# Three of seven pairs of up blocks with both blocks by seven block products

## The chip, the cores and the metric

The kernel runs on one core of one Trainium2 chip. The metric is the device time of the whole program in microseconds (us); the median over several executions is compared. Engines are named as in the profile: PE (TensorE matmul), PEld (its weight load), DVE (VectorE), ACT (ScalarE), POOL (GpSimd), SP (SyncE, which only issues transfers here).

## The reference

One decoder layer on x of 512 tokens by 1024 features: a mixer (four mLSTM heads and a group of convolutions with a common output projection), then a gated feed-forward part, each between norms that are modulated from the vector c (the "ada" weights). The change lies in the feed-forward part:

```python
u = rms_norm(x, ffn_pre_g[l]) * (1.0 + sc2) + sh2
up = causal_dwconv(u @ ffn_up[l], ffn_conv_w[l], ffn_conv_b[l])      # D_FF = 2816, conv width 3
a, gt = jnp.split(up, 2, axis=-1)
f = (jax.nn.silu(gt) * a) @ ffn_down[l]
x = x + g2 * rms_norm(f, ffn_post_g[l])
```

All of it is float32.

## The kernel before, in words

A float32 product is made of three fast ones: each operand is split into a rounded part (hi) and the rest (lo), and PE runs hi x hi, hi x lo and lo x hi into the same sum. So one 128 x 128 tile of weights against 512 tokens costs three matmuls.

**Up blocks.** The 2816 features of each half of up make 22 blocks of 128. Up block n computes value block n and gate block n for all 512 tokens. A plain block takes 2 halves x 8 tiles x 3 = 48 matmuls of 512 columns (plain_half, lines 188 to 190). Blocks 0 to 7 are plain. Blocks 8 to 21 run in seven pairs, m = 4 to 10, with i = 2m and j = 2m + 1. Of each pair the even block i is computed by a scheme with seven products in place of eight: its weights form a 2 x 2 arrangement (value and gate against the two halves of the 1024 features), its tokens two halves, and seven products p1 to p7 of 12 matmuls of 256 columns each (form_product, L1095) are made of sums of weight quarters and sums of token parts. first_products makes four: p1 in the left and p5 in the right half of a bank X, p7 in Z, p6 in W. between(i) then combines them: two ACT copies (L1111 of X, L1112 of W) and four DVE additions in PSUM (L1113 to L1116). last_products_up adds p2 and p3 to X and p4 to Z. The odd block j is plain: its value half runs between the first four and the last three products of i, its gate half behind them.

**Weights.** up_load fetches the quarters of a block (256 KB each) through SP's queue into one of two raw buffers, wups0 for even and wups1 for odd blocks. A form of a weight is split in one of two ways. w_split: ACT copies the rounded part (L170), POOL subtracts it from the source (L171). added_split: ACT writes the rounded part and its negative (L1086, L1087), and a transfer that POOL issues adds the source to the latter in memory (L1088). The forms of the even block are made in place in the raw quarters by DVE subtractions and additions (before: L1316 for p3, L1349 for p7, L1350 for p5, L1365 for p6), so each of them must wait until the form that was there is split. All splits take tiles of one pool, w, of 20.

**After the products.** conv3 convolves a half over tokens (L997 on ACT, L999 on DVE), unit_out makes F = value x silu(gate) (L1141 ACT, L1142 DVE), form_sums (L1024 to L1027), form_highs (L1032) and form_lows (L1038) prepare F of the pair before for the down products. ada_fetch and ada_add (L1146, L1151) put four blocks of the last modulation into pairs 5 to 8; four more (L153, L155) run ahead of the up blocks. After pair 8 ada_done (L160) and gain (L667) finish that modulation.

**Order.** In the pairs nothing is reordered: the code is under in_order(), so that DVE, ACT and POOL each run their instructions in the order in which the loop issues them, and PE and SP always do. An engine that waits at one instruction holds up all behind it. PE's banks: four for X and Z or plain blocks ("mm"), two for W ("at"), two for plain halves of j ("cv").

**Down products** follow with the same scheme; at the end last_products(2) and (3) make the last p4 of blocks m = 8, 9, 10 for the two token halves q (prod2, L1465), whose weight forms t_8, t_9, t_10 are split just ahead (L1015, L1016).

## Time and profile before

| | us |
|---|---|
| three executions | 768.56, 769.04, 771.67 (median 769.04) |
| the profiled execution | 769.46 |
| its span, first to last instruction | 767.7 |
| PE busy in the span | 753.0 |
| first matmul of pair 8/9 to that of pair 10/11 (528.76 to 549.76) | 21.00 |

The rows of the profile come from one execution: start and duration in us, engine, line, operation, tile names, and in brackets the idle time ahead with what ended it. The groups and the page give totals. The first matmul of a pair is told by the tile upx. Mean granted clock of PE is 0.997.

### The profile page before, as it was taken

The numbers are of one execution on the slowest core, as the hardware profiler recorded it, in microseconds if no ns is written. First come the engines' busy times: TensorE is split into PE (matmuls) and PEld (weight loads), VectorE is DVE, ScalarE is ACT, GpSimd is POOL, SyncE is SP. The second block draws the span as 40 slices with busy tenths as digits, with TensorE's granted clock in tenths as the row PEclk, the third lists the DMA queues.
The fourth block names the chain that finished last, engine by engine and source line by source line (L and its number), as shares of the span: only waits on it lengthen the run. The fifth ranks groups of instructions, "written<-read, shape, count | busy, mean of one in ns | idle before, by whom it ended". The sixth has DMA issues, their size and how long they took to land.

```text
span 767.7 us, 11547 instructions
## 1 busy us (share of the span) xinstructions
PE 753.0 (98%) x3961; PEld 644.1 (84%) x3961; DVE 640.2 (83%) x1034; ACT 449.9 (59%) x860; POOL 367.2 (48%) x320
## 2 busy tenths in 40 slices
PE   7999999999999999999999999999999999999996
PEld 5778898778888888988888998889998988888884
DVE  6997999999999966765768789877787878999986
ACT  5448257676766547582244566677676667546653
POOL 2029578696798735433661435455565554100001
PEclk9999999999999999999999999999999999999998
DMA  8983214203123453334953679899788879899692
GB/s 322 370 309 122 102 55 165 82 29 127 61 86 112 138 183 118 139 117 155 382 180 129 241 186 237 204 251 231 207 202 194 214 204 225 258 356 373 225 335 109
DMA packets 55999, 148.47 MB, mean 193 GB/s; under 512 B 6370, under 2 KB 7810, under 8 KB 51844
## 3 DMA queue, kind: packets, MB, share of 16 engines
q1 hardware_dynamic: 33588, 100.37, 37.9%
q10 hardware_dynamic: 14288, 32.68, 12.3%
q0 software_dynamic: 8064, 14.68, 11.1%
q8 instruction: 31, 0.51, 0.3%
q14 instruction: 28, 0.23, 0.1%
HBM read 117.42 MB, written 15.61 MB: 173 GB/s over the span
## 4 chain that ended last, share of the span: by engine, by line
PE 67%; DVE 22%; DMA 6%; ACT 2%; issue 2%; POOL 1%; ACTq 0%; DVEq 0%; POOLq 0%; SPq 0%
DVE cv L731 10%; PE up L190 7%; PE up L189 7%; PE up L188 7%; PE upx L1095 4%; PE glu L189 3%; PE glu L190 3%; PE glu L188 3%; PE p L1465 3%; PE p L189 3%; PE p L188 3%; PE p L190 3%; PE upz L1095 2%; PE mixa L188 2%; PE mixa L190 2%
## 5 line engine op out<-in xcount | busy, mean ns | idle before, releaser
L731 DVE SCALAR_TENSOR_TENSOR cv<-gt,cvw,cv 128x505 f32<-128x505 f32 (+24 forms) x200 | 137.3, 729 | 2.3 <-ACT cv L719 1.1
L727 POOL TENSOR_TENSOR cs<-cs,cs 128x510 f32<-128x510 f32 (+3 forms) x32 | 41.8, 1306 | 0.3
L685 POOL TENSOR_TENSOR ro2r<-ro2t,mhalf 128x1 f32<-128x1 f32 x1 | 0.6, 562 | 82.7 <-DVE ro2t L683 82.7
L725 ACT ACTIVATE cs<-gt,cvw 128x511 f32<-128x511 f32 (+4 forms) x40 | 27.5, 720 | 5.9 <-POOL cs L727 2.7
L155 DVE SCALAR_TENSOR_TENSOR junk<-ada,cb 128x1024 bf16<-128x1024 f32 x16 | 24.9, 1559 | 7.2 <-DMA ada<-in_adaT 7.0
L189 PE MATMUL up<-u2l,wup_0h 128*128 128x512 f32 (+1 forms) x72 | 25.7, 356 | 0.2 <-DVE u2l L910 0.2
L188 PE MATMUL up<-u2h,wup_0h 128*128 128x512 f32 (+1 forms) x72 | 25.6, 356 | 0.0
L190 PE MATMUL up<-u2h,wup_0l 128*128 128x512 f32 (+1 forms) x72 | 25.4, 353 | 0.0
L171 POOL TENSOR_TENSOR wglu_0l<-wglu,wglu_0h 128x512 fp32r<-128x512 f32 x4 | 5.5, 1382 | 41.3 <-PE glu L190 41.3
L171 POOL TENSOR_TENSOR wqko_1024l<-wqko,wqko_1024h 128x512 fp32r<-128x512 f32 x12 | 15.6, 1296 | 18.3 <-ACT wqko_1024h L170 12.9
L155 DVE SCALAR_TENSOR_TENSOR junk<-spare,cb 128x1024 bf16<-128x1024 f32 x12 | 18.6, 1548 | 4.1 <-DMA spare<-in_adaT 3.9
L188 PE MATMUL qko<-uh,wqko_1024h 128*128 128x512 f32 x48 | 20.6, 430 | 0.0
L188 PE MATMUL qko<-uh,wqko_0h 128*128 128x512 f32 x48 | 20.2, 420 | 0.0
L276 DVE SCALAR_TENSOR_TENSOR junk<-ada,cb 128x1024 bf16<-128x1024 f32 x16 | 19.5, 1220 | 0.1
L171 POOL TENSOR_TENSOR wo_512l<-wo,wo_512h 128x512 fp32r<-128x512 f32 x8 | 12.9, 1614 | 13.7 <-PE mixa L189 11.5
L171 POOL TENSOR_TENSOR wqko_0l<-wqko,wqko_0h 128x512 fp32r<-128x512 f32 x12 | 16.6, 1384 | 4.9 <-ACT wqko_0h L170 4.9
L190 PE MATMUL qko<-uh,wqko_1024l 128*128 128x512 f32 x48 | 18.8, 392 | 0.0
L171 POOL TENSOR_TENSOR wqko_512l<-wqko,wqko_512h 128x512 fp32r<-128x512 f32 x12 | 17.0, 1419 | 3.7 <-ACT wqko_512h L170 3.7
L190 PE MATMUL qko<-uh,wqko_0l 128*128 128x512 f32 x48 | 18.8, 391 | 0.0
L171 POOL TENSOR_TENSOR wo_1024l<-wo,wo_1024h 128x512 fp32r<-128x512 f32 x8 | 11.7, 1456 | 14.9 <-ACT wo_1024h L170 14.9
L189 PE MATMUL qko<-ul,wqko_1024h 128*128 128x512 f32 x48 | 18.7, 390 | 0.0
L189 PE MATMUL qko<-ul,wqko_0h 128*128 128x512 f32 x48 | 18.7, 390 | 0.0
(1239 smaller groups left out, 3118.5 us busy)
## 6 DMA issues: line engine op xcount, KB each, us to landing
wups<-in_w_up SPq DMA_DIRECT2D x56, 256.0 KB, 4.8
wqko<-in_w_qko SPq DMA_DIRECT2D x12, 1024.0 KB, 4.7
ada<-in_adaT ACTq DMA_DIRECT2D x20, 512.0 KB, 4.4
ada<-in_adaT SPq DMA_DIRECT2D x16, 512.0 KB, 6.8
wo<-in_w_out SPq DMA_DIRECT2D x8, 1024.0 KB, 4.8
wup<-in_w_up SPq DMA_DIRECT2D x8, 1024.0 KB, 6.9
spare<-in_adaT ACTq DMA_DIRECT2D x12, 512.0 KB, 7.6
wd<-in_w_down SPq DMA_DIRECT2D x20, 256.0 KB, 5.7
```

The costliest lines, as they stand in the source:

```text
L155: t = V.scalar_tensor_tensor(out=junk, in0=r, scalar=1.0, in1=cb, op0=ALU.mult, op1=ALU.mult, accum_out=mod[:, i : i + 1])
L171: (eng or G).tensor_tensor(out=lo[:, :n], in0=src, in1=hi[:, :n].bitcast(F32), op=ALU.subtract)
L188: PE.matmul(ps, a[0], b[0], start=start, stop=False)
L189: PE.matmul(ps, a[0], b[1], start=False, stop=False)
L190: PE.matmul(ps, a[1], b[0], start=False, stop=stop)
L276: V.scalar_tensor_tensor(out=junk, in0=first[k][:, i * D : (i + 1) * D], scalar=1.0, in1=cb, op0=ALU.mult, op1=ALU.mult, accum_out=part[k] ...
L685: G.tensor_tensor(out=r, in0=t, in1=mhalf[:, :1], op=ALU.pow)
L725: S.activation(t[:, d:], cvx[j][:, : T - d], AF.Copy, scale=w(CK - 1 - d))
L727: G.tensor_tensor(out=side[:, d:], in0=side[:, d:], in1=t[:, d:], op=ALU.add)
L731: last_tap[0] = V.scalar_tensor_tensor(out=cp[:, d:], in0=cvx[j][:, : T - d], scalar=w(CK - 1 - d), in1=cp[:, d:], op0=ALU.mult, op1=ALU.add)
L1095: PE.matmul(ps, x, y, start=start and k == 0 and n == 0, stop=stop and k == NT - 1 and n == 2, skip_group_check=True)
L1465: PE.matmul(ps[q], x, y, start=False, stop=m == NM - 1 and i == 2, skip_group_check=True)
```

## The change

In pairs 5, 7 and 9 (BOTH) the odd block j is computed by seven products too, with its X and Z in the two cv banks. PE's order in such a pair is four products of i, four of j, three of i, three of j. The forms of j (L1321, L1322, L1333, L1354) are new DVE operations, and between(j) runs a second time. Of i, p4 and p3 change from w_split to added_split in these pairs; p2, p4 and p3 of j are added_split, p7, p5 and p6 of j w_split, and p1 of j is split at the end of the pair before. The convolution of j's value half moves to the next pair, beside that of its gate half. up_load runs in another order. Two ada blocks (44, 45) move ahead of the up blocks, the other two are fetched in pairs 6 and 8. In pair 10 the first down weights are split behind quarter 2 of j in place of ahead of it. At the end the p4 products of the last two token tiles run in another order.

```diff
@@ -978,7 +978,7 @@
         turn_out(2)
         up_split(2, raw2, wpool, "w")
         turn_out(3)
-    for n in range(40, 44):
+    for n in range(40, 46):
         ada_block(n, last_lo[0])
     up_half(0, 2, 1)
     for i in range(NE):
@@ -1096,8 +1096,8 @@
 
     sforms = {}
 
-    def first_products(i):
-        X, Z, W = mmbank(f"upx{i}"), mmbank(f"upz{i}"), atbank(f"upw{i}")
+    def first_products(i, bank=mmbank):
+        X, Z, W = bank(f"upx{i}"), bank(f"upz{i}"), atbank(f"upw{i}")
         w = sforms[i]
         form_product(X[:, :HT], w["p1"], B11, True, False)
         form_product(Z[:, :HT], w["p7"], tforms["t3"], True, False)
@@ -1157,6 +1157,7 @@
 
     g2 = []
     MS = SUNITS[0] // 2
+    BOTH = (MS + 1, MS + 3, MS + 5)
     Fs = {}
 
     def open_F(m):
@@ -1311,29 +1312,53 @@
             banks = first_products(i)
             if not more_to_come:
                 load1(1, [slot(f"wd1_1_{b}") for b in range(4)])
-            pa = plain_half(cvbank(f"up{j}_0"), value, 0)
             s4 = slot(f"s4_{m}")
             V.tensor_tensor(out=s4, in0=a12, in1=a11, op=ALU.subtract)
             weight_form(i, "p2", a12, added_split)
-            weight_form(i, "p4", a22)
+            weight_form(i, "p4", a22, added_split if m in BOTH else w_split)
+            if m in BOTH:
+                b11, b12, b21, b22 = places(j)
+                V.tensor_tensor(out=b11, in0=b11, in1=b21, op=ALU.subtract)
+                V.tensor_tensor(out=b21, in0=b21, in1=b22, op=ALU.add)
             bj, ba, bg = before
-            bg = conv3(bg, NF + bj, f"fg{bj}")
-            weight_form(i, "p3", s4)
-            if not more_to_come:
-                part_b(0)
-            if more_to_come:
-                for n, q in ((i, 2), (i, 0), (j, 0), (i, 3), (j, 1), (i, 1)):
-                    up_load(n + 2, (q,))
-            unit_out(bj, ba, bg, Fs[m - 1])
-            gate = [value_part(j, 2)]
+            if ba is None:
+                ba, bg = (conv3(ps, n, f"f{n}c") for ps, n in zip(bg, (bj, NF + bj)))
+            else:
+                bg = conv3(bg, NF + bj, f"fg{bj}")
+            weight_form(i, "p3", s4, added_split if m in BOTH else w_split)
+            if m in BOTH:
+                weight_form(j, "p7", b11)
+                weight_form(j, "p5", b21)
+                unit_out(bj, ba, bg, Fs[m - 1])
+                V.tensor_tensor(out=b11, in0=b22, in1=b11, op=ALU.subtract)
+                weight_form(j, "p6", b11)
+                for q in (2, 0, 3, 1):
+                    up_load(i + 2, (q,))
+                others = first_products(j, cvbank)
+            else:
+                pa = plain_half(cvbank(f"up{j}_0"), value, 0)
+                if more_to_come:
+                    for n, q in ((i, 2), (i, 0), (j, 0), (i, 3), (j, 1), (i, 1)):
+                        up_load(n + 2, (q,))
+                unit_out(bj, ba, bg, Fs[m - 1])
+                gate = [value_part(j, 2)]
+                if not more_to_come:
+                    part_b(0)
             form_sums(m - 1, Fs[m - 1])
             between(i, *banks)
             if not more_to_come:
                 forms1(0)
                 load1(2)
-            gate.append(value_part(j, 3))
-            if more_to_come:
-                up_load(j + 2, (2, 3))
+            if m in BOTH:
+                s4 = slot(f"s4_{m}j")
+                V.tensor_tensor(out=s4, in0=b12, in1=b11, op=ALU.subtract)
+                for name, z in (("p2", b12), ("p4", b22), ("p3", s4)):
+                    weight_form(j, name, z, added_split)
+                up_load(j + 2, (0, 2, 1, 3))
+            else:
+                gate.append(value_part(j, 3))
+                if more_to_come:
+                    up_load(j + 2, (2, 3))
             form_highs(m - 1, Fs[m - 1])
             if more_to_come:
                 form_lows(m - 1, Fs[m - 1])
@@ -1350,7 +1375,7 @@
                 V.tensor_tensor(out=a21, in0=a21, in1=a22, op=ALU.add)
             else:
                 part_b(1)
-            va = conv3(pa, j, f"fa{j}")
+            va = None if m in BOTH else conv3(pa, j, f"fa{j}")
             if not more_to_come:
                 parts1(0)
                 forms1(1)
@@ -1359,24 +1384,33 @@
             if more_to_come:
                 weight_form(i + 2, "p7", a11)
                 weight_form(i + 2, "p5", a21)
-                value = [value_part(j + 2, 0)]
-                if MS < m < MS + 5:
-                    ada = ada_fetch(m + 39)
+                if m + 1 not in BOTH:
+                    value = [value_part(j + 2, 0)]
+                if m in (MS + 2, MS + 4):
+                    ada = ada_fetch(m // 2 + 43)
                 V.tensor_tensor(out=a11, in0=a22, in1=a11, op=ALU.subtract)
             if m - 1 < SPILLED:
                 own_out(m - 1)
             X, Z, _ = banks
             last_products_up(X, Z, sforms[i])
-            pg = plain_half(cvbank(f"up{j}_1"), gate, 0)
+            if m in BOTH:
+                between(j, *others)
+                last_products_up(*others[:2], sforms[j])
+                pg = others[:2]
+            else:
+                pg = plain_half(cvbank(f"up{j}_1"), gate, 0)
             vx, vz = conv3(X, i, f"fa{i}"), conv3(Z, NF + i, f"fg{i}")
             if not more_to_come:
                 parts1(1, 0, 2)
             if more_to_come:
                 weight_form(i + 2, "p6", a11)
-                value.append(value_part(j + 2, 1))
+                if m + 1 in BOTH:
+                    weight_form(j + 2, "p1", places(j + 2)[0])
+                else:
+                    value.append(value_part(j + 2, 1))
             unit_out(i, vx, vz, Fs[m])
-            if MS < m < MS + 5:
-                ada_add(m + 39, ada)
+            if m in (MS + 2, MS + 4):
+                ada_add(m // 2 + 43, ada)
             if m == MS + 4:
                 ada_done(40, 48)
                 gain(3, 40, "ffn_post_g")
@@ -1491,9 +1525,13 @@
                     for q in range(2):
                         prod2(n, which, q)
     def last_products(tt):
-        for which in ("p2", "p3") if tt < 2 else ("p4",):
-            for m in range(M2, NM):
-                prod2(m, which, tt % 2)
+        if tt < 2:
+            for which in ("p2", "p3"):
+                for m in range(M2, NM):
+                    prod2(m, which, tt)
+        else:
+            for m, q in ((M2, 0), (M2 + 1, 0), (M2, 1), (M2 + 2, 0)) if tt == 2 else ((M2 + 1, 1), (M2 + 2, 1)):
+                prod2(m, "p4", q)
 
     def last(tt, hf):
```

ACT in pair 10/11 from between's copies to the next pair's splits; p15_10 and p15_11 are between's copies for i and j, wups0 and wups1 the raw buffers, wup12 and wup13 the next pair's forms (13_0: quarter 0 of the plain block 13). Before, two rows behind the copies of between(10):

```order
L1032 ACTIVATE fh4_0_5527<-F4_5153 128x512
L1032 ACTIVATE fh4_1_5529<-ysum_1376 128x512
L1033 DMA g2d4_4547<-F4_5153 128x512
L1034 DMA g2d4_4547<-ysq_1377 128x256
L170 ACTIVATE wup12_p1h_5537<-wups0_5100 128x512
L997 ACTIVATE fa11c_5543<-up11_0_5451,vec_111 128x512
L170 ACTIVATE wup12_p7h_5547<-wups0_5100 128x512
L170 ACTIVATE wup12_p5h_5551<-wups0_5100 128x512
L1086 ACTIVATE wup13_0h_5555<-wups1_5101 128x512
L1087 ACTIVATE wup13_0l_5556<-wups1_5101 128x512
```

Now, from p3 of block 11 to between(11):

```order
L1087 ACTIVATE wup11_p3l_5571<-s4_5j_5558 128x512
L1032 ACTIVATE fh4_0_5579<-F4_5161 128x512
L1032 ACTIVATE fh4_1_5581<-ysum_1376 128x512
L1033 DMA g2d4_4555<-F4_5161 128x512
L1034 DMA g2d4_4555<-ysq_1377 128x256
L170 ACTIVATE wup12_p1h_5589<-wups0_5108 128x512
L170 ACTIVATE wup12_p7h_5595<-wups0_5108 128x512
L170 ACTIVATE wup12_p5h_5599<-wups0_5108 128x512
L1086 ACTIVATE wup13_0h_5603<-wups1_5109 128x512
L1087 ACTIVATE wup13_0l_5604<-wups1_5109 128x512
L1111 ACTIVATE p15_11_5645<-upx11_5495 128x256
L1112 ACTIVATE p15_11_5645<-upw11_5497 128x256
```

What moved: the two copies of between(11) stand behind p1, p7 and p5 of block 12 and both copies of quarter 0 of block 13; the convolution fa11c is gone from here.

DVE in the first part of pair 10/11, before (from s4 of i to between(i)):

```order
L1316 TENSOR_TENSOR s4_5_5476<-wups0_5100 128x512
L999 SCALAR_TENSOR_TENSOR fg9c_5487<-up9_1_5355,vec_111,fg9c_5487 128x511
L999 SCALAR_TENSOR_TENSOR fg9c_5487<-up9_1_5355,vec_111,fg9c_5487 128x510
L1142 TENSOR_TENSOR F4_5153<-fa9c_5297,fg9c_5487 128x512
L1024 TENSOR_TENSOR ysum_1376<-F4_5153 128x256
L1025 TENSOR_TENSOR F4_5153<-F4_5153 128x256
L1026 TENSOR_TENSOR ysum_1376<-ysum_1376,F4_5153 128x256
L1027 TENSOR_TENSOR ysq_1377<-F4_5153,ysum_1376 128x256
L1113 TENSOR_TENSOR u2_10_5513<-upx10_5400,p15_10_5512 128x256
L1114 TENSOR_TENSOR upz10_5401<-upz10_5401,u2_10_5513 128x256
L1115 TENSOR_TENSOR upx10_5400<-upx10_5400,u2_10_5513 128x256
L1116 TENSOR_TENSOR upz10_5401<-upz10_5401,p15_10_5512 128x256
```

Now:

```order
L1316 TENSOR_TENSOR s4_5_5453<-wups0_5108 128x512
L1321 TENSOR_TENSOR wups1_5109<-wups1_5109 128x512
L1322 TENSOR_TENSOR wups1_5109<-wups1_5109 128x512
L999 SCALAR_TENSOR_TENSOR fg9c_5467<-up9_1_5358,vec_111,fg9c_5467 128x511
L999 SCALAR_TENSOR_TENSOR fg9c_5467<-up9_1_5358,vec_111,fg9c_5467 128x510
L1142 TENSOR_TENSOR F4_5161<-fa9c_5305,fg9c_5467 128x512
L1333 TENSOR_TENSOR wups1_5109<-wups1_5109 128x512
L1024 TENSOR_TENSOR ysum_1376<-F4_5161 128x256
L1025 TENSOR_TENSOR F4_5161<-F4_5161 128x256
L1026 TENSOR_TENSOR ysum_1376<-ysum_1376,F4_5161 128x256
L1027 TENSOR_TENSOR ysq_1377<-F4_5161,ysum_1376 128x256
```

What moved: L1321 and L1322 (the forms p7 and p5 of j) come ahead of fg9c, and L1333 (p6 of j, which overwrites what L1321 made) between F and form_sums.

DVE in the second part, now, from s4 of j to between(j):

```order
L1354 TENSOR_TENSOR s4_5j_5558<-wups1_5109 128x512
L1038 TENSOR_TENSOR fl4_0_5580<-F4_5161,fh4_0_5579 128x512
L1038 TENSOR_TENSOR fl4_1_5582<-ysum_1376,fh4_1_5581 128x512
L1374 TENSOR_TENSOR wups0_5108<-wups0_5108 128x512
L1375 TENSOR_TENSOR wups0_5108<-wups0_5108 128x512
L1391 TENSOR_TENSOR wups0_5108<-wups0_5108 128x512
L1113 TENSOR_TENSOR u2_11_5646<-upx11_5495,p15_11_5645 128x256
L1114 TENSOR_TENSOR upz11_5496<-upz11_5496,u2_11_5646 128x256
L1115 TENSOR_TENSOR upx11_5495<-upx11_5495,u2_11_5646 128x256
```

L1374, L1375 and L1391 are before's L1349, L1350 and L1365, the forms p7, p5 and p6 of block 12 in place of one another in wups0; between(11) is behind them.

## Prediction

> **What bounds the kernel now.** The page first, then the waits of PE from 440 us to the end, then one pair of up blocks in windows. In the page's rows the last column but one is the count of instructions; PEclk and DMA shares stand behind the busy times of a window.
>
> ```profile
> span 767.7 us, 11547 instructions
> PE 753.0 (98%) x3961; PEld 644.1 (84%) x3961; DVE 640.2 (83%) x1034; ACT 449.9 (59%) x860; POOL 367.2 (48%) x320
> q0 software_dynamic: 8064, 14.68, 11.1%
> wups<-in_w_up SPq DMA_DIRECT2D x56, 256.0 KB, 4.8
> ...
> PE up L190 <- DMA wup_2l<-wups: 0.4, 1, 0.4
> PE p L1465 <- DVE t_10l L1016: 0.2, 1, 0.2
> ...
> 570.76:591.76 21.00, 21.00 (x134) 19.08 (x134) 16.69 (x27) 14.65 (x26) 12.16 (x11) 1.00 0.83 207
> 612.76:634.00 21.24, 21.24 (x136) 19.22 (x136) 16.61 (x28) 12.34 (x22) 11.71 (x11) 1.00 0.75 191
> ...
> 507.60:513.35 5.75, 5.75 (x50) 1.00 0.97 199
> 513.35:518.82 5.47, 5.47 (x27) 1.00 1.04 285
> 518.82:523.13 4.31, 4.31 (x38) 1.00 0.67 180
> 523.13:528.60 5.47, 5.47 (x27) 1.00 1.05 269
> ```
>
> PE is busy for 98% of the span, and in a whole pair (21.00 us) for all of it, with DVE at 16.69, ACT at 14.65 and POOL at 12.16. After 440 us it waits twice, 0.4 and 0.2 us. So PE's own work sets the time here, and the other four queues matter only if one of them comes later than PE. The last four rows cut pair 8/9 in the order of before: the four products of i, half of plain j, the three products of i, the other half of j.
>
> **What PE saves.** Seven products take 5.75 + 4.31 = 10.06 us, a plain block 2 x 5.47 = 10.94. Each of the three blocks that change saves 0.88 us, all three 2.6.
>
> **When PE now wants the odd block's sums.** PE's order becomes four (i) 5.75, four (j) 5.75, three (i) 4.31, three (j). The last three of j add to the banks that between(j) rewrites, so its adds L1113 to L1115 must be done 15.81 us after the pair's first matmul. In ACT's queue the two copies that open between(j) stand behind five copies for the next pair (p1, p7, p5 of block i+2 and quarter 0 of block j+2, hi and minus hi). These are to be timed; rows of pair 14/15, which begins at 570.76:
>
> ```profile
> 576.55 0.39 ACT L1112 ACTIVATE p<-upw 128x256 f32<-128x256 f32 x1 [1.05 <-PE upw L1095]
> 576.83 0.62 ACT L1086 ACTIVATE wup_3h<-wups 128x512 fp32r<-128x512 f32 x1
> 577.35 0.62 ACT L1087 ACTIVATE wup_3l<-wups 128x512 fp32r<-128x512 f32 x1
> 578.92 0.62 ACT L170 ACTIVATE wup_p1h<-wups 128x512 fp32r<-128x512 f32 x1
> ...
> 576.97 0.43 DVE L1113 TENSOR_TENSOR u<-upx,p 128x256 f32<-128x256 f32 x1 [0.42 <-ACT p L1112]
> 577.84 0.42 DVE L1115 TENSOR_TENSOR upx<-upx,u 128x256 f32<-128x256 f32 x1
> 578.17 0.42 DVE L1116 TENSOR_TENSOR upz<-upz,p 128x256 f32<-128x256 f32 x1
> 581.00 0.69 DVE L1349 TENSOR_TENSOR wups<-wups 128x512 f32<-128x512 f32 x1 [1.18 <-POOL wup_p1l L171]
> 581.73 0.69 DVE L1350 TENSOR_TENSOR wups<-wups 128x512 f32<-128x512 f32 x1
> ...
> 579.62 1.34 POOL L171 TENSOR_TENSOR wup_p1l<-wups,wup_p1h 128x512 fp32r<-128x512 f32 x1
> 583.39 1.30 POOL L171 TENSOR_TENSOR wup_p7l<-wups,wup_p7h 128x512 fp32r<-128x512 f32 x1 [2.42 <-ACT wup_p7h L170]
> 584.64 1.30 POOL L171 TENSOR_TENSOR wup_p5l<-wups,wup_p5h 128x512 fp32r<-128x512 f32 x1
> ```
>
> Walk, in us after the pair's first matmul, if nothing blocks anything. The copy of W ends at 6.18 (576.55 + 0.39 - 570.76) and between(i) at 7.83 (L1116). The new subtraction s4 of j (0.69, as L1349) ends at 8.5. ACT meanwhile copies p2 and p4 of j (four at a pitch of 0.52: 577.35 - 576.83), then p3 from 8.5 (two, it needs s4), fh (two): p1 of i+2 starts at 10.6. From that copy to L1349 the row shows 2.08 us (581.00 - 578.92), the POOL subtraction between them; then L1350 0.73 later: these two end at 13.35 and 14.1. They feed the copies p7 and p5 of i+2. So p5 starts at 14.1, quarter 0 takes two more copies, and between(j)'s copies start at 15.65 and 16.0; from the start of the second to the end of L1115 the rows show 1.71 us (577.84 + 0.42 - 576.55). PE can go on at 17.7: **a stall of 1.9 us** where 0.88 is saved.
>
> **What blocks on top.** DVE and POOL hold each other up:
>
> ```profile
> 456.50 5.33 POOL L1061 TENSOR_TENSOR b<-u2h,u2l 128x512 f32<-128x512 f32 x4
> 456.96 5.43 DVE L1038 TENSOR_TENSOR fl<-F,fh 128x512 fp32r<-128x512 f32 x1
> ...
> L1365 DVE TENSOR_TENSOR wups<-wups 128x512 f32<-128x512 f32 x3 | 5.3, 1766 | 1.1 <-POOL wup_p7l L171 1.1
> L1350 DVE TENSOR_TENSOR wups<-wups 128x512 f32<-128x512 f32 x3 | 2.1, 693 | 0.1
> ...
> 584.73 1.77 DVE L1365 TENSOR_TENSOR wups<-wups 128x512 f32<-128x512 f32 x1 [0.36 <-POOL wup_p7l L171]
> 573.90 0.93 DVE L1142 TENSOR_TENSOR F<-fa13c,fg13c 128x512 f32<-128x512 f32 x1 [0.76 <-ACT fg13c L1141]
> ```
>
> A DVE operation of 0.69 us took 5.43 while four POOL subtractions ran, and L1365 takes 1766 ns where the same form in L1350 takes 693: it starts under p5's POOL subtraction (584.64 to 585.94) and ends 0.56 after it. The Trainium skill says the same ("SBUF — State Buffer", "Who interferes with whom"): a DVE operation with two SBUF inputs and a GpSimd operation that reads SBUF exclude each other, and whichever issued first holds the port to its end. Operations that read PSUM (L1113 to L1116, 0.42 to 0.43) are not slowed. By the page's rule, who comes first keeps the port, each race goes as in the walk to 6.0 below, and the sum would be 788.
>
> The form of p6 that answers to L1365 in the change stands directly ahead of L1113 of j. By the row it ends 0.56 after p5's subtraction: p7's starts 0.70 after its copy (579.62 - 578.92) at 14.05, p5's follows to 16.65, L1113 starts at 17.2, L1115 ends 1.29 later (577.84 + 0.42 - 576.97), at 18.5: **2.7 us of stall**.
>
> The early part of the pair gets it too: three POOL subtractions (p7, p5, p6 of j, 1.3 each) now fall between F (L1142), the change's third subtraction for p6, and form_sums (L1024 to L1027). F waits for p7's (to 4.6) and ends at 5.1; p5's then starts at 5.1, to 6.4; the subtraction for p6 waits until then, to 7.0. ACT's copy p6 of j stands ahead of W's copy of i, which ends at 8.2 in place of 6.18. p6's POOL subtraction runs to 9.05, form_sums finish at 9.8, between(i) at 11.2, s4 of j at 11.9 (for 8.5). p1 of i+2 starts at 14.0; its POOL subtraction shares the port with fl (L1038) and ends at 16.2; L1349's and L1350's like to 17.6; p7's POOL subtraction 17.6 to 18.9, p5's to 20.1, L1365's like to 20.7, L1115 at 21.8: **6.0 us**. If DVE wins one of the races for 1.3 us, 4.6. I take 5.3 for the first two pairs.
>
> The third pair starts later: mod and gains for the last ada blocks stand ahead of its first DVE operation.
>
> ```profile
> 590.75 1.22 DVE L1151 SCALAR_TENSOR_TENSOR junk<-ada,cb 128x1024 bf16<-128x1024 f32 x1
> 613.01 2.02 DVE L160 TENSOR_TENSOR mod<-mod,vec 128x8 f32<-128x8 f32 x1
> ```
>
> L160 took 2.02 us for eight columns, with p4's subtraction on POOL beside it, which the change takes away; the stall grows by something between nothing and 2.0, and I take 1.3: 6.6. The three stalls make 17.2 (15.1 to 19.3).
>
> **PE's clock after a stall.** Before never stalls so long in the middle, but its end shows what idleness does; the last matmul starts at 760.58:
>
> ```profile
> 760.58 0.39 PE L1465 MATMUL p<-b_10h,s 128*128 128x512 f32 x1
> ...
> 762.00:763.00 1.00, 0.00 (x0) 0.97 0.00 0
> 763.00:764.00 1.00, 0.00 (x0) 0.50 0.00 0
> ```
>
> The granted clock falls to 0.50 about 2 us after the last matmul. No row shows how it returns. A stall of 5 us should meet it; one of 1.9 may not. Bounds: nothing, or half speed for as long as the stall (5.3 us at half lose 2.65). I take a return as quick as the fall: 2.0 us at half, 1.0 lost, 3.0 for three. The Trainium skill ("TensorE: Matmul & The Clock Gate", "What's actually happening") gives about 3.4 us of work before the clock is full again, an estimate of 1.7 lost each; by it this term would be 5.1.
>
> **The rest.** (a) Pair 20/21: the DMA part of down block 0 moves behind that of quarter 2, so PE's 0.4 goes. (b) The tail:
>
> ```profile
> 749.29 0.49 PE L1465 MATMUL p<-t_10h,g2h 128*128 128x512 f32 x1
> 750.02 0.50 PE L1465 MATMUL p<-t_10l,g2h 128*128 128x512 f32 x1 [0.23 <-DVE t_10l L1016]
> 750.59 0.39 PE L1465 MATMUL p<-t_8h,g2h 128*128 128x512 f32 x1
> 750.82 0.40 PE L1465 MATMUL p<-t_8l,g2h 128*128 128x512 f32 x1
> ```
>
> At a pitch of 0.23 the three products of t_10 would take 0.69; they take 1.30 (750.59 - 749.29). Three matmuls of block 8 now come first, 0.69 later is enough for t_10l: -0.6, at least the 0.2 of the wait. (c) Two ada blocks go to the loop before the up blocks, where the waits show PE waiting for nothing from 440 on: nothing; without that cover, two DVE operations like L1151, 2.4. (d) DVE has eight operations more in such a pair, 4 x 0.69 + 4 x 0.42, and no L1151: 16.69 + 4.4 - 1.2 = 19.9 of the 20.1 that PE's work lasts, so nothing that is late can be caught up. They are in the walk. (e) p4 and p3 of i become a second copy on ACT and an accumulating transfer each, in place of a POOL subtraction; like p2 they are wanted from 11.5 on.
>
> ```profile
> wup_p2l<-wups POOLq DMA_DIRECT2D x7, 256.0 KB, 4.2
> ```
>
> Issued at about 3 at the latest, they land by 7 to 8: nothing. Those of j, issued between 10 and 13.6 in the walk to 6.0, land between 14.2 and 17.8, before the stall ends: nothing, and C if they are slower. The loads' new order on SP puts all four of block i+2 first and quarter 0 of block j+2 behind s4 of j; the first have half a pair, the last is C's.
>
> **Sum**, on the profiled execution's 769.46 (0.4 above the median, 769.04): -2.6 + 17.2 + 3.0 - 0.4 - 0.6 = +16.6: 786.
>
> **Rivals.** *A, the blocking does not compound*: DVE's operations slip in between POOL's, and only the queue order is left: 1.9 to 2.7 a pair, 1.3 more in the third, no lower clock: 7.0 to 9.4 - 3.6: 773 to 775. For it: L1142 lost only 0.24 in the row. Against it: L1365 lost its 1.07 in all three pairs of its group.
> *B, not slower*: ACT reaches between(j)'s copies by about 14.1, so that L1115 ends by 15.81. Then all of -3.6 stays: 765.9. It decides from p1 of i+2 starting at 8.7 or earlier instead of 10.6. For it: ACT is busy for only 14.65 of 21 us. Against it: W's copy ends at 6.18 at the earliest and eight copies at 0.52 follow before p1, to 10.3.
> *C, transfers late too*: 56 accumulating transfers take 11.1% of the span, 1.5 us each of all engines (0.111 x 767.7 / 56). The pair issues eight in place of five and drops an ada load (0.83 to 0.75 in the windows): 0.83 + 4.5 / 21 - 0.08 = 0.96. Quarter 0 of j+2 is loaded only after s4 of j (11.9 + 4.8 = 16.7, wanted at 18.2); a load 3 us slower than its median adds 1.5 a pair, with p3 of j as much again at most: 790 to 795.
>
> **Chances.** Forecast 0.55 (own range 781 to 793), A 0.20, B 0.10, C 0.15. From 0.5% on (3.8 us, about what a measurement of this kernel tells from no change) I count: B ends 0.4% below, so it is split between same and faster; A at its low end borders on the same. Slower 0.84, same 0.11, faster 0.05. Range 771 to 793: it reaches down through A and leaves out B and most of C's upper end.
>
> **What would show it.** Three PE waits of 4 to 7 us on upx of blocks 11, 15 and 19, released by DVE L1115; ahead of them in ACT the copies p7 and p5 of the next even block; the operation like L1365 at 1.7 us or more; the subtraction for p6 near 1.9; granted clock under 1.00 right after the stall; 0.4 and 0.2 gone from PE's waits. Stalls near 2 us speak for A, none for B, a release by a DMA for C. Wrong would be a wait elsewhere, in a plain pair above all.

## The result and the profile after

The changed kernel takes 797.16 us (median of 4 runs, 796.05 to 797.45) against 768.8 before: a ratio of 1.037, 95% interval 1.0352 to 1.0388. It is slower, as forecast, but by 28 us in place of 17, and lies above the range of 771 to 793. Its profiled execution took 796.05 us with a span of 794.3, 26.6 more than before's 767.7.

The page of the change, and PE's waits from 430 to 700 us (what PE waited for: us in total, times, longest):

```profile
span 794.3 us, 11839 instructions
PE 757.2 (95%) x4069; PEld 653.4 (82%) x4069; DVE 659.8 (83%) x1058; ACT 455.4 (57%) x878; POOL 377.8 (48%) x329
...
PE upx L1095 <- DVE upx L1115: 21.5, 4, 7.8
PE upw L1095 <- POOL wup_p6l L171: 1.0, 1, 1.0
PE up L188 <- DVE fa7c L999: 0.4, 1, 0.4
```

PE waited for 0.4 us in this stretch before; now for 22.9, nearly all of it for DVE's L1115, the third addition of between. The stretches from one pair's first matmul to the next pair's (windows of the change: us, then busy time and instructions of PE, PEld, DVE, ACT, POOL, then PEclk and the transfers; pair 16/17, like 12/13, is left out):

```profile
507.56:530.53 22.97, 21.45 (x133) 19.06 (x132) 19.35 (x29) 16.31 (x30) 14.30 (x13) 1.00 0.85 229
530.53:561.31 30.78, 23.23 (x169) 22.44 (x168) 22.35 (x33) 20.57 (x39) 18.17 (x18) 0.89 0.66 154
561.31:582.32 21.01, 21.01 (x135) 19.09 (x133) 16.47 (x26) 12.89 (x24) 10.53 (x10) 1.00 0.67 179
582.32:610.14 27.82, 21.66 (x170) 21.49 (x169) 20.93 (x33) 18.20 (x36) 16.58 (x16) 0.88 0.73 166
631.14:660.97 29.83, 22.04 (x171) 21.84 (x169) 21.39 (x36) 18.71 (x36) 16.74 (x17) 0.89 0.79 199
660.97:794.30 133.33, 125.89 (x596) 105.62 (x594) 117.13 (x197) 73.30 (x144) 11.18 (x14) 0.99 0.78 261
```

Before, these stretches took 21.00 five times, 21.10 and 134.00. So the 26.6 us are: +1.97 in pair 8/9, whose own two blocks are computed as before; +9.78, +6.82 and +8.73 in the three changed pairs; -0.67 at the end; nothing in pairs 12/13 and 16/17. Among the pairs, PE's clock is below 1.00 in the changed ones only.

The stall itself, pair 14/15 (first matmul at 582.32; DVE, ACT and PE of the change):

```profile
586.88 2.14 DVE L1142 TENSOR_TENSOR F<-fa13c,fg13c 128x512 f32<-128x512 f32 x1 [0.76 <-ACT fg13c L1141]
588.94 0.68 DVE L1333 TENSOR_TENSOR wups<-wups 128x512 f32<-128x512 f32 x1
590.78 1.40 DVE L1027 TENSOR_TENSOR ysq<-F,ysum 128x256 f32<-128x256 f32 x1
593.63 0.68 DVE L1354 TENSOR_TENSOR s_7j<-wups 128x512 f32<-128x512 f32 x1
596.51 0.62 ACT L170 ACTIVATE wup_p1h<-wups 128x512 fp32r<-128x512 f32 x1
601.38 1.74 DVE L1391 TENSOR_TENSOR wups<-wups 128x512 f32<-128x512 f32 x1 [1.38 <-POOL wup_p7l L171]
603.90 0.42 DVE L1115 TENSOR_TENSOR upx<-upx,u 128x256 f32<-128x256 f32 x1
604.47 0.55 PE L1095 MATMUL upx<-u2h,wup_p2h 128*128 128x256 f32 x1 [6.16 <-DVE upx L1115]
```

Against the prediction's walk to 6.0 (offsets from 582.32): the subtraction for p6 ends at 7.3 (walk: 7.0), s4 of j at 12.0 (11.9), p1 of the next block starts at 14.2 (14.0), L1115 ends at 22.0 (21.8). F takes 2.14 in place of 0.69 while two POOL subtractions run (585.59 to 588.47), ysq 1.40 in place of 0.42 beside a third, the operation like L1365 1.74. L1333 itself, which the prediction saw near 1.9, takes 0.68: F had done the waiting.

And the clock there (windows of PE alone, the change):

```profile
600.00:601.00 1.00, 0.00 (x0) 0.78 1.11 349
601.00:602.00 1.00, 0.00 (x0) 0.50 1.13 215
...
604.47:607.17 2.70, 2.70 (x13) 0.50 0.65 127
```

Twelve products of p2 take 2.70 us in place of 1.44. The clock fell at about 600.6, 2.3 us after the last matmul, and was full again at 607.4, 2.9 us after PE went on.

### The profile page after: what moved, and what is told of

The parts are those of the page before. It is cut to its first block, busy times and chain, and to the rows that moved or that the text cites. A ratio compares the mean times of both kernels' runs of the same rounds, so it can differ in the third digit from the quotient of the medians.

```text
span 794.3 us, 11839 instructions
## 1 busy us (share of the span) xinstructions
PE 757.2 (95%) x4069; PEld 653.4 (82%) x4069; DVE 659.8 (83%) x1058; ACT 455.4 (57%) x878; POOL 377.8 (48%) x329
## 4 chain that ended last, share of the span: by engine, by line
PE 56%; DVE 25%; ACT 6%; DMA 4%; issue 4%; POOL 2%; ACTq 1%; POOLq 0%; DVEq 0%
DVE cv L731 7%; PE p L1499 4%; PE upx L1095 3%; PE glu L189 3%; PE qko L188 3%; PE qko L190 3%; PE qko L189 3%; PE glu L190 3%; PE glu L188 3%; PE p L188 3%; PE p L189 3%; PE p L190 3%; PE mixa L190 2%; PE mixa L188 2%; PE mixa L189 2%
## 5 line engine op out<-in xcount | busy, mean ns | idle before, releaser
L1095 PE MATMUL upx<-u2h,wup_p2h 128*128 128x256 f32 x40 | 13.5, 339 | 21.6 <-DVE upx L1115 21.5
L155 DVE SCALAR_TENSOR_TENSOR junk<-ada,cb 128x1024 bf16<-128x1024 f32 x18 | 27.7, 1540 | 4.6 <-DMA ada<-in_adaT 4.4
L1095 PEld LDWEIGHTS upx<-u2h,wup_p2h 128*128 128x128 f32 x40 | 9.2, 229 | 22.8 <-ACT wup_p6h L170 20.9
L171 POOL TENSOR_TENSOR wqko_1024l<-wqko,wqko_1024h 128x512 fp32r<-128x512 f32 x12 | 16.6, 1381 | 17.1 <-ACT wqko_1024h L170 11.8
L171 POOL TENSOR_TENSOR wup_p6l<-wups,wup_p6h 128x512 fp32r<-128x512 f32 x10 | 13.4, 1344 | 19.5 <-ACT wup_p6h L170 17.5
L188 PE MATMUL up<-u2h,wup_0h 128*128 128x512 f32 (+1 forms) x60 | 21.0, 350 | 0.4 <-DVE fa7c L999 0.4
L189 PE MATMUL up<-u2l,wup_0h 128*128 128x512 f32 (+1 forms) x60 | 20.9, 349 | 0.2 <-DVE u2l L910 0.2
L190 PE MATMUL up<-u2h,wup_0l 128*128 128x512 f32 (+1 forms) x60 | 20.8, 346 | 0.0
L171 POOL TENSOR_TENSOR wup_p7l<-wups,wup_p7h 128x512 fp32r<-128x512 f32 x10 | 13.9, 1389 | 13.5 <-ACT wup_p7h L170 13.5
L276 DVE SCALAR_TENSOR_TENSOR junk<-ada,cb 128x1024 bf16<-128x1024 f32 x16 | 19.5, 1220 | 0.1
```

What stands on the lines that cost most here:

```text
L155: t = V.scalar_tensor_tensor(out=junk, in0=r, scalar=1.0, in1=cb, op0=ALU.mult, op1=ALU.mult, accum_out=mod[:, i : i + 1])
L171: (eng or G).tensor_tensor(out=lo[:, :n], in0=src, in1=hi[:, :n].bitcast(F32), op=ALU.subtract)
L188: PE.matmul(ps, a[0], b[0], start=start, stop=False)
L189: PE.matmul(ps, a[0], b[1], start=False, stop=False)
L190: PE.matmul(ps, a[1], b[0], start=False, stop=stop)
L276: V.scalar_tensor_tensor(out=junk, in0=first[k][:, i * D : (i + 1) * D], scalar=1.0, in1=cb, op0=ALU.mult, op1=ALU.mult, accum_out=part[k] ...
```

## The experiments

Each run was compared with the kernel before on the same chip (768.74 in the runs e1 to e4, 768.93 in e5 to e8, 768.04 in e9 to e12). The length of each pair, from the first matmul of p1 (tile upx) to the next pair's, in us:

| run | median | 8/9 | 10/11 | 12/13 | 14/15 | 16/17 | 18/19 |
|---|---|---|---|---|---|---|---|
| before | 768.8 | 21.00 | 21.00 | 21.00 | 21.00 | 21.00 | 21.10 |
| the change | 797.16 | 22.97 | 30.78 | 21.01 | 27.82 | 21.00 | 29.83 |
| e1, ada as before | 792.82 | 21.01 | 28.11 | 21.01 | 29.25 | 21.01 | 30.43 |
| e2, ada moved alone | 770.50 | 23.06 | 21.00 | 21.00 | 21.00 | 21.00 | 21.10 |
| e3, end alone | 769.33 | 21.00 | 21.00 | 21.00 | 21.00 | 21.00 | 21.11 |
| e4, between(j) early | 792.77 | 23.04 | 26.53 | 21.12 | 27.54 | 21.01 | 25.92 |
| e5, no POOL for j | 788.19 | 22.93 | 27.46 | 21.01 | 26.34 | 21.01 | 27.51 |
| e6, no POOL for i+2 | 790.32 | 22.45 | 29.07 | 21.01 | 26.51 | 21.01 | 27.54 |
| e7, neither | 778.83 | 22.74 | 25.02 | 21.04 | 22.02 | 21.01 | 25.14 |
| e8, j from i's forms | 775.28 | 21.00 | 20.66 | 21.01 | 20.41 | 21.01 | 29.15 |
| e9, row late | 794.85 | 23.01 | 30.86 | 21.01 | 27.89 | 21.01 | 29.09 |
| e10, PE kept busy | 794.00 | 23.05 | 28.73 | 21.01 | 26.78 | 21.01 | 31.09 |
| e11, one pair | 776.72 | 21.00 | 21.00 | 21.00 | 28.40 | 21.01 | 21.11 |
| e12, transfers alone | 770.46 | 21.00 | 21.00 | 21.00 | 21.00 | 21.00 | 21.11 |

**e1 and e2: where do the 2 us of pair 8/9 come from?** e1 takes one part out of the change, e2 puts the same part alone into the kernel before:

```diff
-    for n in range(40, 46):
+    for n in range(40, 44):          # e1, in the change; e2 is the reverse, in before
         ada_block(n, last_lo[0])
-                if m in (MS + 2, MS + 4):
-                    ada = ada_fetch(m // 2 + 43)
+                if MS < m < MS + 5:
+                    ada = ada_fetch(m + 39)
```

> The change with the ada blocks where they were before (four ahead of the up blocks, 44 to 47 fetched in pairs 5 to 8), all else as in the change. Theory one (the two ada blocks moved ahead make DVE and ACT about 2 us late from block 2 on, and they stay late up to the first changed pair): pair 8/9 goes back from 22.97 to about 21.0 us, the 1.0 us wait on wup_p6l in pair 10/11 goes, its stall is some 0.5 us shorter: 797 falls to about 793.5, less up to 1.2 us for a DVE operation that comes back. Theory two (the pairs themselves make pair 8/9 late, by its new loads and splits): pair 8/9 stays at 23 us and the time at 797.

> The kernel before with nothing but the move of the two ada blocks. Theory one (ada makes DVE late): pair 8/9 takes about 23 us in place of 21.0, PE waits there for DVE by some 1.5 us, and the time is about 771. Theory two: 769, no PE wait between 500 and 530 us.

Measured: e1 792.82 us (ratio 1.0313, interval 1.0295 to 1.033), pair 8/9 at 21.01, the wait on wup_p6l gone, pair 10/11 2.7 shorter. e2 770.50 (1.0022, 1.0009 to 1.0036), pair 8/9 at 23.06 and these two waits, in a kernel without any changed pair (PE, e2):

```profile
513.78 0.47 PE L188 MATMUL up<-u2h,wup_0h 128*128 128x512 f32 x1 [0.46 <-DVE fa7c L999]
520.60 0.35 PE L1095 MATMUL upx<-u2h,wup_p2h 128*128 128x256 f32 x1 [1.12 <-DVE upx L1115]
```

So it is the ada move. How two operations of 1.2 us at 450 us become a wait at 513 is seen in DVE and POOL. Before:

```profile
464.21 1.53 DVE L999 SCALAR_TENSOR_TENSOR fa3c<-up,vec,fa3c 128x511 f32<-128x511 f32 x2 [0.62 <-ACT fa3c L997]
475.22 5.70 DVE L1027 TENSOR_TENSOR ysq<-F,ysum 128x256 f32<-128x256 f32 x1
475.27 5.36 POOL L1061 TENSOR_TENSOR b<-u2h,u2l 128x512 f32<-128x512 f32 x4
482.11 0.68 DVE L1038 TENSOR_TENSOR fl<-ysum,fh 128x512 fp32r<-128x512 f32 x1
511.73 0.92 DVE L1142 TENSOR_TENSOR F<-fa7c,fg7c 128x512 f32<-128x512 f32 x1 [0.76 <-ACT fg7c L1141]
```

The change:

```profile
467.31 1.53 DVE L999 SCALAR_TENSOR_TENSOR fa3c<-up,vec,fa3c 128x511 f32<-128x511 f32 x2 [1.65 <-ACT fa3c L997]
481.19 0.88 POOL L1088 DMA_DIRECT2D wup_0l<-wup  x1 [3.34 <-ACT wup_0l L1087]
481.34 6.34 DVE L1038 TENSOR_TENSOR fl<-ysum,fh 128x512 fp32r<-128x512 f32 x1 [0.35 <-ACT fh L1032]
481.77 5.36 POOL L1061 TENSOR_TENSOR b<-u2h,u2l 128x512 f32<-128x512 f32 x4
516.69 0.92 DVE L1142 TENSOR_TENSOR F<-fa7c,fg7c 128x512 f32<-128x512 f32 x1 [0.76 <-ACT fg7c L1141]
```

DVE is 3.1 us late at 464 and 5.0 late at 512. In between, both kernels have a DVE operation held by a row of four POOL additions (L1061, token_forms; the prediction took such a row for subtractions): ysq before, until 480.9, and fl in the change, until 487.7. The row starts 6.5 us later now. Before it ran ahead of POOL's transfer for wup_0l (at 483.41), now behind it, and that transfer waited 3.34 us for ACT. The plain blocks are not under in_order(), so the ada move also changed the order of instructions there (e2 has POOL's new order, e1 the old one). How much of the 2 us is the two operations and how much the new order, no run tells apart. PE waited for nothing from 440 to 507 us in before, but DVE had little slack, and what is late there reaches PE only at 513.

In e1 pairs 14/15 and 18/19 are longer than in the change (29.25 and 30.43 for 27.82 and 29.83), with the same stalls within 0.3 (6.44 and 7.84 for 6.16 and 7.79): the rest is the clock, which came back 5.3 and 4.8 us after PE went on in place of 2.9 and 3.6.

**e3: the end and pair 20/21.** Before, with the last p4 products in the new order and the first down weights split behind quarter 2:

```diff
-        for which in ("p2", "p3") if tt < 2 else ("p4",):
-            for m in range(M2, NM):
-                prod2(m, which, tt % 2)
+            for m, q in ((M2, 0), (M2 + 1, 0), (M2, 1), (M2 + 2, 0)) if tt == 2 else ((M2 + 1, 1), (M2 + 2, 1)):
+                prod2(m, "p4", q)
...
             gate = [value_part(j, 2)]
+            if not more_to_come:
+                part_b(0)
```

> The kernel before with nothing but the last p4 products in the new order and the first down weights of pair 20/21 split behind quarter 2. By the terms of the prediction: the 0.4 us wait on wup_2l and 0.2 to 0.6 us at t_10l go, so 0.6 to 1.0 us less than before: 767.8 to 768.2. Rival: the waits come back elsewhere in the chain (another DMA, the next form's split) and the time stays within 0.2 us of before.

Measured: 769.33 us, 1.0004 (0.9991 to 1.0017): no gain that can be told, at most 0.1%. The 0.4 us on wup_2l is gone, but (one of PE's waits of e3, and DVE and PE at the end):

```profile
PE p L1465 <- DVE t_2l L1016: 0.3, 1, 0.3
...
748.77 0.69 DVE L1254 TENSOR_TENSOR wdmore<-wdmore 128x512 f32<-128x512 f32 x1 [0.76 <-DMA wdmore<-t2d]
750.99 0.50 PE L1465 MATMUL p<-t_10l,g2h 128*128 128x512 f32 x1 [0.23 <-DVE t_10l L1016]
```

A new wait of 0.3 appears at t_2l, and t_10l is waited for as long as before: DVE's L1254 waits for a transfer that comes at 748.8 in place of 747.8. What sets PE's wait is not the split alone but the transfer ahead of it, and the transfer moved; why it did is not shown. In the change itself, where all is later, neither wait shows, and the end is 0.67 shorter.

**e4: only the order of the queues?** The change with between(j) issued right behind the splits of j:

```diff
                 up_load(j + 2, (0, 2, 1, 3))
+                between(j, *others)
...
-                between(j, *others)
                 last_products_up(*others[:2], sforms[j])
```

> The change with between(j) issued ahead of form_highs and of the next pair's forms on ACT and DVE. Theory A (queue order alone makes the stall): the three stalls of 6 to 8 us on upx L1115 vanish, with them the lower clock (5.2 us lost), and what takes their place is small: 797 - 21 - 5 = about 771. Theory B (DVE and POOL, which shut each other out, have no time left in such a pair): the stalls move to the next pair, where the plain half of j+2 waits for a bank that the convolution of j frees late, and the next pair's forms come late, 1 to 4 us each, some 13 to 20 us in all; only the clock gains, since no stall is long: 786 to 793.

Measured: 792.77 us, 1.0313 (1.0296 to 1.033), theory B's total. PE's four longest waits from 430 to 700 us:

```profile
PE upx L1095 <- DMA wup_p3l<-s_7j: 3.9, 1, 3.9
PE upx L1095 <- DMA wup_p3l<-s_9j: 3.2, 1, 3.2
PE up L188 <- DVE f19cc L999: 3.1, 1, 3.1
PE upx L1095 <- DMA wup_p3l<-s_5j: 2.9, 1, 2.9
```

The adds of the changed pairs are in time now, and three waits on wup_p6l make 2.5 us; what PE waits for next is p3 of j, whose transfer POOL issues only after s4 of j and which takes 6.3 to 7.4 us to land. This is rival C's transfer, hidden in the change behind a longer stall: theory B named the next pair's bank as the place, which shows only once, in pair 20/21 (3.1). A stall of 2.9 us still halved the clock, from 0.95 us after PE had gone on.

**e5, e6, e7: does POOL block DVE?** The POOL subtraction of a split is left out and the rounded part taken for the rest; e5 for p7, p5 and p6 of j, e6 for p1, p7 and p5 of i+2, e7 for all six, in the changed pairs. The outputs leave out these rests.

```diff
+    def half_split(src, name):
+        hi = wpool.tile([P, T], F32R, tag="w", name=f"{name}h")
+        S.activation(hi, src, AF.Copy)
+        return hi, hi
...
-                weight_form(j, "p7", b11)
+                weight_form(j, "p7", b11, half_split)
```

> The change without the three POOL subtractions for p7, p5 and p6 of j in the changed pairs; PE takes the rounded part in place of the rest, so that all its matmuls run, but the output leaves out the rests of these forms. Theory of mutual blocking: F (L1142) takes 0.7 in place of 2.1 us, s4 of j comes 2.5 to 3.4 us earlier, and each stall of 6.2 to 7.8 falls to 3 to 5; with less time at the low clock the run takes 784 to 788 in place of 797. Rival (only the order of the queues on ACT and DVE delays between(j); POOL is idle before p1 of i+2 anyway): stalls unchanged, 797.

> The change without the POOL subtractions for p1, p7 and p5 of block i+2 in the changed pairs, the rounded part taken for the rest as above; the output leaves out the rests of these forms. Theory: the subtractions L1374 and L1375 no longer wait 1.3 us for POOL, and the one like L1391 takes 0.7 in place of 1.74: 2 to 2.4 us off each stall, 3.9 to 5.4 left, 788 to 790. Rival (these lie beside ACT's own copies, which are as late): under 1 us off each, 794 or more.

> Both together: in the changed pairs all six of these POOL subtractions are left out (and their rests from the output). If the two parts of the walk add: stalls of 0.7 to 1.7 in pairs 10/11 and 14/15 and about 3.4 in 18/19, hardly any low clock: 769 + 0.9 (ada) - 2.6 + 6 = 771 to 775. If the queue order keeps the 1.9 us a pair of the walk without blocking: 775 to 777. If something else than POOL delays these pairs: over 785.

Measured: 788.19 us (1.0242, 1.0219 to 1.0265), 790.32 (1.0276, 1.0255 to 1.0298) and 778.83 (1.0133, 1.0118 to 1.0148). The stall of pair 14/15, PE of e5 (with two rows of DVE), e6 and e7:

```profile
583.72 0.69 DVE L1147 TENSOR_TENSOR F<-fa13c,fg13c 128x512 f32<-128x512 f32 x1 [0.76 <-ACT fg13c L1146]
586.18 0.42 DVE L1027 TENSOR_TENSOR ysq<-F,ysum 128x256 f32<-128x256 f32 x1
598.79 0.55 PE L1100 MATMUL upx<-u2h,wup_p2h 128*128 128x256 f32 x1 [3.63 <-DVE upx L1120]
```

```profile
600.06 0.36 PE L1100 MATMUL upx<-u2h,wup_p2h 128*128 128x256 f32 x1 [4.65 <-ACT fg14c L997]
```

```profile
593.33 0.36 PE L1100 MATMUL upx<-u2h,wup_p2h 128*128 128x256 f32 x1 [1.65 <-ACT fg14c L997]
```

From 6.16 us: 2.5 off without j's subtractions, 1.5 off without those of i+2, 4.5 off without either. (L1120 is the same addition, five lines down, and L1147 is F; where the row names ACT's convolution, that ended 0.02 us behind the addition.) The other two stalls, 6.44 and 7.79 in the change, became 5.12 and 5.31 in e5, 4.99 and 5.77 in e6, 3.14 and 3.35 in e7; so e5 and e6 missed some of the stalls forecast, by up to 0.4 us. In e7 what is left in 14/15, 1.65, comes near the queue order of the walk without blocking (1.9). The mutual blocking is thus shown for j's subtractions: F and ysq read nothing that these make, and without them they take 0.69 and 0.42 us, not 2.14 and 1.40. In e6 the wait of L1374 for p1's subtraction goes too, and the two are not told apart. e7's total lies above both forecasts: pair 8/9 keeps 1.7 us of the ada move, and the stalls of 10/11 and 18/19 lower the clock. Why the stall of 10/11 is 1.5 us longer than that of 14/15 is not shown.

**e8: what PE saves.** The change with ada as before and the products of j made from i's weight forms, so that none of j's forms is made; the output is not the reference's in these blocks.

```diff
             if m in BOTH:
-                b11, b12, b21, b22 = places(j)
-                V.tensor_tensor(out=b11, in0=b11, in1=b21, op=ALU.subtract)
-                V.tensor_tensor(out=b21, in0=b21, in1=b22, op=ALU.add)
+                sforms[j] = sforms[i]
```

> The change with the ada blocks as before and with the products of j made from the weight forms of i: all forms of j are left out (four DVE operations, its ACT copies, POOL subtractions and transfers), so the output is not the reference's in these blocks; PE runs the same matmuls in the same order and between(j) stays where it is. If PE's saving is 0.88 us a block and the forms of j are what makes between(j) late: pairs 10/11 and 14/15 take 20.1 us each without a wait, 18/19 has a wait of about 3.6: 769 - 2.6 + 3.6 - 0.6 = 769 to 771. Rival (the order alone, between(j) behind the forms of i+2, as in the walk without blocking): stalls of about 1.9 in each of the three, 771 to 774.

Measured: 775.28 us (1.0079, 1.0062 to 1.0097). Pair 14/15, in PE's order four (i), four (j), three (i), three (j):

```profile
569.11:574.86 5.75, 5.75 (x49) 1.00 0.76 150
574.86:580.62 5.76, 5.76 (x50) 1.00 0.98 284
580.62:584.93 4.31, 4.31 (x38) 1.00 0.82 262
584.93:589.52 4.59, 4.59 (x38) 1.00 0.47 100
```

PE's part is as predicted to 0.3 us, which is lost at the first product behind between(j) (in pair 10/11 a wait of 0.25 stands at the same matmul). So the forms of j and not the order alone make between(j) late: without them the same order is in time by all but this. Pair 18/19 missed, and with it the total, which lies above both forecasts: a stall of 5.9 in place of 3.6, with a low clock behind it. There ACT and DVE show (e8):

```profile
622.35 0.28 DVE L655 COPY gTs<-gT 8x128 f32<-8x128 f32 x1 [2.63 <-PE gT L653]
624.52 0.29 ACTq L657 DMA_DIRECT2D row_d<-gTs  x1
624.86 0.63 ACT L170 ACTIVATE wup_p1h<-wups 128x512 fp32r<-128x512 f32 x1 [6.95 <-DMA g2d<-ysq]
```

ACT stood for 6.95 us ahead of p1 of block 20, behind the transfer of the last modulation row (send_rows), for which PE turns the gains only behind the four products of j.

**e9: the third pair's longer stall.** The change with send_rows behind the products of that pair:

```diff
             if m == NM - 2:
-                send_rows(3 * KT, KT)
                 early_raw = adas.tile([P, D], F32, tag="ada", name="wd1_0")
...
             vx, vz = conv3(X, i, f"fa{i}"), conv3(Z, NF + i, f"fg{i}")
+            if m == NM - 2:
+                send_rows(3 * KT, KT)
```

> The change with the last modulation row sent (a PE transposition, a DVE copy, a transfer in ACT's queue) behind the products of pair 18/19 in place of ahead of p1 of block 20. Theory one (this row, which stands ahead of that copy in ACT's queue, makes the third stall longer than the others): the wait of 7.8 us in pair 18/19 falls to about 6.3 like the other two; the run takes 795 to 796.5, since the row may cost some of it in pair 20/21. Theory two (it is mod and gains, as the prediction had it, or the saved time of POOL): 7.8 stays.

Measured: 794.85 us (1.0354, 1.033 to 1.0378). PE in pair 18/19:

```profile
653.94 0.55 PE L1095 MATMUL upx<-u2h,wup_p2h 128*128 128x256 f32 x1 [6.44 <-DVE upx L1115]
```

7.79 becomes 6.44, the others' length: theory one. It gives 1.1 of it back at a bank in pair 20/21 (a wait of PE for DVE f19cc). What the prediction blamed, L160, takes 0.17 us in the change.

**e10: the clock by itself.** 48 matmuls whose result nothing uses stand in the stall of pairs 10/11 and 14/15:

```diff
                 between(j, *others)
+                for k in range(48 if m < NM - 2 else 0):
+                    PE.matmul(banks[2][:, HT:], sforms[i]["p2"][0][:, :P], B21[k % NT][0], start=True, stop=True, skip_group_check=True)
                 last_products_up(*others[:2], sforms[j])
```

> The change with 48 matmuls of 256 columns, whose result nothing uses, between the three products of i and those of j in pairs 10/11 and 14/15; they read what lies ready and take 5.8 us. Theory one (the idle stretch itself halves the granted clock, and the low clock costs 2.2 and 1.4 us there): PE's clock stays 1.00 in both pairs, the waits there shrink to under 1 us, and the run falls by 3 to 4 us, to 793 to 794. Theory two (the matmuls behind the stall are slow because transfers or DVE hold them up): the three products of j stay at 5.2 us and the time at 797 or above.

Measured: 794.00 us (1.0323, 1.0298 to 1.0348), 3.2 below the change. Pair 14/15 of e10 (the three products of j run from 603.01):

```profile
603.01 0.36 PE L1095 MATMUL upx<-u2h,wup_p2h 128*128 128x256 f32 x1 [0.64 <-DVE upx L1115]
...
604.00:605.00 1.00, 1.00 (x10) 1.00 0.54 94
```

The clock stays at 1.00, and the two pairs are 2.05 and 1.04 shorter. So it is idleness that halves the clock, and matmuls that do nothing are enough to keep it. Pair 18/19, which has none of them, took 1.26 us longer than in the change behind nearly the same stall (7.84 for 7.79), and the two profiled executions differ by 1.5 us only.

**e11: does it add up over the pairs?** e1 with one changed pair alone:

```diff
-    BOTH = (MS + 1, MS + 3, MS + 5)
+    BOTH = (MS + 3,)
```

> The change in one pair alone, 14/15, with the ada blocks as before. Theory one (each changed pair pays for itself, nothing is carried on): pair 14/15 takes 27.8 to 29.3 us as in the change with all three, all others 21.0, and the run takes 768.9 + 7 to 8 = 776 to 777. Theory two (what is late adds up over the pairs): its stall is 1 us or more shorter than 6.2, the run under 775.

Measured: 776.72 us (1.0111, 1.009 to 1.0131); pair 14/15 takes 28.40 with a stall of 6.2, all others 21.0. Each pair pays for itself.

**e12: parts of i by transfers alone**, in the kernel before:

```diff
-            weight_form(i, "p4", a22)
+            weight_form(i, "p4", a22, added_split if m in (MS + 1, MS + 3, MS + 5) else w_split)
```

(and the same for p3.)

> The kernel before with nothing but p4 and p3 of i by a second copy on ACT and a transfer in place of POOL's subtraction, in pairs 10/11, 14/15 and 18/19. The prediction has this at nothing: 768.9, no wait of PE there. Rival (the transfers land late, or hold up others): waits of PE on wup_p4l or wup_p3l or on parts of the plain block, 770 or more.

Measured: 770.46 us, 1.0034 (1.0019 to 1.0049), which is the rival's time. But the profiled execution took 769.4 with all pairs as before and no wait of PE on these parts, so the rival's waits are not there. The profile agrees with the prediction's nothing; where the median loses its 1.5 to 3.8 us it does not show, and this stays open.

No version here beats the kernel before.

## Why the prediction was right and wrong

Right: the direction and the chain. Three long waits on upx of blocks 11, 15 and 19 for L1115, behind the next pair's splits in ACT's queue and behind DVE operations that POOL holds up (e5, e7), with a lower clock after each (e10), and PE's saving of 0.88 a block (e8). The sum failed by its sizes; by its own terms, for the 26.6 us of the profiled executions:

| term | predicted | measured |
|---|---|---|
| PE's saving, three blocks | -2.6 | -2.6 (a pair takes 20.12 without its waits; e8) |
| stalls on L1115 | 5.3, 5.3, 6.6 | 6.4, 6.2, 7.8 (20.9 from matmul to matmul) |
| lower clock | 1.0 each | 2.2, 1.3, 1.6 |
| ada move (c) | 0 | 2.0 in pair 8/9, 1.8 in 10/11 (30.78 less the terms above; 1.0 of it is the wait on wup_p6l, gone in e1) |
| wait on wup_2l, and the end | -1.0 | -0.7 |
| sum | 16.6 | 26.5 |

- *The stall.* The walk gave 6.0 and I entered 5.3, halfway to a case in which DVE wins a race with POOL for 1.3 us. It won none: F waited for both subtractions (2.14) and not for one, and the end of the walk held to 0.2 us. The discount of 0.7 cost 2.1 us over the three pairs; another 1.6 (20.9 less 19.3) the walk did not have. The sentence weighed beside it, that who comes first keeps the port ("SBUF — State Buffer", "Who interferes with whom", the Trainium skill), gave the better number: its 788 came nearer than 786. The rows bear out that an operation waits to the end of POOL's, but not that the first to start wins (last section).
- *The third pair.* The 1.3 us more were there (1.4 to 1.6), but by luck, for another reason: send_rows, which stands in three queues ahead of p1 (e8, e9), and not mod and gains. I had not followed what else ACT's queue holds there.
- *The clock.* "A return as quick as the fall" was wrong: it fell 2.3 us after the last matmul in pair 14/15, and came back 2.9 us after PE went on there, 4.8 and 3.6 in the other two pairs: 5.1 us lost over the three in place of 3.0. The Trainium skill's figure ("TensorE: Matmul & The Clock Gate", "What's actually happening"), 3.4 us of work, gave 5.1 as an estimate. Its sum is what the trace shows, in part by luck: the loss was 1.3 to 2.2 us, and in e10 pair 18/19 lost 1.2 more behind nearly the same stall.
- *The ada move.* This is the term that was wrong in kind. The prediction named a wait in a plain pair as the sign of being wrong, and pair 8/9 has it (1.14 and 0.37 us). I looked at PE's waits from 440 on and found none, and called it cover. DVE, of which I quoted no window, had little to spare behind the place where they go (DVE of before; 3.0 of the 9.86 us are an fl that stands beside POOL's first row of additions):

```profile
450.00:460.00 10.00, 9.86 (x13) 1.00 0.78 173
```

Lateness there grew from 3.1 to 5.0 us past POOL's next row, which came 6.5 us later in a new order (e2). The edit should have been followed on DVE, in the order that the changed kernel has, up to the next thing that PE takes from it.
- *The end.* Both waits were real and small; e3 shows that alone they are not to be had, since a transfer sets them.

Rival A is excluded by the stalls of 6 us and more, B by L1115 of j, which ended 22.0 us into the pair and not by 15.81; e4 and e8 show what B would have needed: an earlier between(j) meets late transfers, and only a kernel that makes no forms of j is in time. Rival C did not happen in the change but stands right behind it (e4).

## What to carry to other kernels

Where a walk through the queues gives a number from rows, that number belongs in the sum; a discount for luck in races needs a row that shows such luck. An edit that puts work on an engine with idle time still has to be followed to that engine's next deadline, above all where two engines shut each other out. Where nothing fixes the order of instructions, the order of the changed kernel has to be compared too: here a move of two blocks reordered POOL. And a saving on the bounding engine of 0.9 us a step is worth nothing if the others have not as much to spare: here DVE, POOL and the transfers would each have needed it.

## What the runs showed of the hardware

- DVE operations with both inputs in SBUF and POOL additions or subtractions do not run side by side: an operation of 0.68 took 6.34 beside four of them, 2.14 beside two, and one of 0.42 took 1.40 beside one. L1116, which reads PSUM, kept its 0.42 beside one (at 604.23 in the change, POOL from 604.27). By their starts fl (481.34 in the change) and ysq (475.22 before) began 0.43 and 0.05 us ahead of POOL's row and were held all the same, so these rows do not show that the first to start wins; starts on POOL are rough.
- PE's granted clock fell to 0.50 some 1.9 to 5.1 us after the last matmul ahead of a stall (in six stalls of 2.9 to 4.7 us, in e4, e6 and e7, 0.2 to 1.3 us after PE had gone on). The stall of 1.65 in e7 did not lower it.
- The low stretch comes in fixed lengths, whatever PE does in it. Read from windows of 0.25 us (a mean of 0.62 is low for 76% of its window), it lasted 6.83 us in all three stalls of the change and in eleven more in e1, e5, e6, e9 and e11, 3.41 in four of e4, one of e6 and two of e7, and 10.24 in one each of e1, e8 and e10: one, two or three times 3.41. Pair 14/15 of the change, where it fell and where it rose:

```profile
600.50:600.75 0.25, 0.00 (x0) 0.62 1.24 377
607.25:607.50 0.25, 0.25 (x3) 0.73 1.26 213
```

The Trainium skill gives a window of 3413 ns that runs freely, whatever a kernel does ("TensorE: Matmul & The Clock Gate", "What's actually happening"); these lengths agree with it, and so do the places: the clock of the change fell at 552.78, 600.56 and 651.76 (windows 552.75:553.00 at 0.55, 651.75:652.00 at 0.52), which is 14.0 and 15.0 times 3.41 apart. So what a stall costs on top of its length hangs on where in that window it begins: 1.3 to 2.2 us in the change, for stalls of 6.2 to 7.8, and 2.4 in e5 for one of 3.6 (26.34 less 20.12 and 3.79 from matmul to matmul).
- Matmuls that nothing uses keep the clock at 1.00 through a stall (e10).
